# A two-layer mLSTM and retention trunk on one core: the same operations, put in order by a planner with other durations

## The chip, the cores and the metric

The kernel runs on one core of a Trainium2 chip (trn2). A core has a matrix engine (PE, with its weight loads shown as PEld), a vector engine (DVE), a scalar engine (ACT), a general engine (POOL) and a queue engine (SP), which here issues every DMA transfer. Each engine carries out its own list of instructions in order; an instruction waits until the semaphores that it names have been raised by others. The metric is the time of one execution on the device in microseconds (us), the median of several runs.

## The reference

Two layers over a sequence of T = 1024 tokens of width D = 1024, and a final RMS norm. All is float32. Per layer, cut to what matters:

```
shift, scale, gate = split(silu(c) @ w_ada[l] + b_ada[l])
h = rmsnorm(x, norm_g[l]) * (1 + scale) + shift
p = h @ w_in[l]                        # 1024 x 1024 by 1024 x 9224
mq, mk, mv, mo, mz, mi, mf, rq, rk, rv, rz = split(p)
mq, mk = silu(causal_conv4([mq, mk]))
y_m = sigmoid(mo) * head_norm(mlstm(mq, mk, mv, mi, mf)) * silu(mz)   # 4 heads of 256
y_r = head_norm(retention(rotary(rq), rotary(rk), rv)) * silu(rz)     # 4 heads of 256
x = x + gate * ([y_m, y_r] @ w_out[l])                                # 2048 x 1024
```

`mlstm` is linear attention with an exponential input gate, a sigmoid forget gate and a running maximum; its gates come from the eight columns `mi, mf`. `retention` is linear attention with a fixed decay per head.

## The kernel before

**Work.** Float32 products are taken as three products of rounded parts: every operand is split into a high part (`hH`, `wH`, `yH`, `oH`, `aH`: a copy by ACT into the matrix engine's 32-bit format) and a low part (`hL`, `wL`, ..: the difference, by DVE or POOL), and `mm3` records high by high, low by high and high by low. The projection `h @ W_in` is done for pairs of 128 columns (`pair`) by a scheme with seven instead of eight block products; the blocks of weights come from memory as `raw` tiles of 128x512, are added and subtracted by DVE and then split. Each finished pair of 128x1024 outputs (`x`) goes through what its columns need: `conv_pair` (convolution and SiLU, for q and k of the mLSTM heads), `rot_pair` (rotary, for q and k of retention), `v_pair`, and `zo_pair` or `z_pair` (gates). The results are stored to memory in `qdr` (q and k), `kdr` and `vdr` (rearranged k and v) and `gdr` (gates, two halves of the sequence), and loaded again where they are used.

**A layer in order.** First the "border": the first gate column block, the values of head group 0 and the eight gate columns (`border_gate`, `border_values`, whose results are gathered in a tile `g8`, shown as `g`), while the normed input of the layer is made. Then `gate_chain`: one long chain of small instructions over the mLSTM gates (scans, a maximum, two transposes of tiles `T4` on PE, exponentials). All mLSTM attention needs its results. Then the pairs of eight head groups (four mLSTM, then four retention); `attention(l, hg)` is recorded as soon as q and k of a group are there. It loads `q` and `kk` from `qdr`, `st` pieces from `vdr` and `kdr`, works in four chunks of 256 tokens with a carried state `cf`, and stores normed outputs `ndr`. Side jobs (`ada_column_job`, `gate_col_job`, `gate_row_job`, `rotary_job`) sum `w_ada` rows on DVE into `aacc` and put them through PE; `gate_row_job` of layer 1 splits `aacc` into `aH` and `aL` and multiplies them by `ones_r`. Last comes `output`: `yr` (from `ndr`) times `yg` (from `gdr`) is split into `yH` and `yL`, and multiplied by `w_out` tiles (`wo`, split into `oH`, `oL`) in two halves of the sequence and two halves of the columns, four 128x512 sums at a time. `evac` of layer 0 loads the residual (`hf<-in_xt_dram`), adds the sum out of its PSUM bank (`hf<-pp,gcol,hf`) and transposes it into `z`; `norm` then makes the next layer's input (`dg`). `evac` of layer 1 adds `xr`, norms and stores the output.

**What sets the order.** The code does not issue instructions where it is written. Every operation is recorded as an `Op` (`Program.record`), with a modelled duration and latency (`cost`), the operations that it depends on (`deps`) and the buffers that it allocates. `Program.order` then plays the whole program through four times (`simulate`): at each step the engine that can start earliest takes an operation. PE takes the earliest of four streams (`pre`, `sums`, `attn`, `main`), each in recorded order; DVE, ACT, POOL and SP take, of the operations whose inputs are there, the one with the smallest `late`, the latest start that the round before left it. A buffer gets a slot of its class when one is free in the model, in recorded order, up to 45 us (`LOOK`) ahead of PE. The best of the four rounds gives the order of all five engines, and the slots. At the end one loop emits all, so that nearly every instruction bears the line of that loop: L1720 in the kernel before, L1743 in the changed one.

```
for op in made:
    getattr(engines[op.eng], op.fn)(*[real(v) for v in op.a], **{n: real(v) for n, v in op.k.items()})
```

An instruction still waits on the chip for what it needs; the planned times are not kept, the order is. 16225 operations are recorded.

## Time and profile before

| | |
|---|---|
| median of 3 runs | 2313.88 us (2313.14 to 2314.32) |
| profiled execution, its own time | 2313.45 us |
| its span, first to last instruction | 2311.7 us |
| mean granted PE clock over the span | 0.974 |
| busy: PE, PEld, DVE, ACT, POOL | 2161.7, 1764.6, 1690.6, 1065.1, 189.4 us |
| DMA | 360.97 MB, mean 156 GB/s |
| table loads on ACT | 23, 1283 ns each |

The profiled execution's own time is 1.75 us above its span and 0.43 us below the median. PE's clock is granted in tenths of full speed; a stretch at half clock makes the same matmuls longer and counts as busy. So PE loses time in two ways: it is idle, or it is busy at a lower clock. The rows of the view by windows name a stretch of the span, then its length, the busy time and instructions of PE, PEld, DVE, ACT and POOL, the granted clock, the busy share of the DMA engines and GB/s. In the timeline a row has its start, its duration, engine, line, operation, out<-in, shapes, the count of equal instructions in a row, and in brackets the idle time before it with what ended it; SPq is the queue that issues the DMAs. PE's single records overlap, so that the pitch from one start to the next is shorter than a record.

### The profile page before, as it was taken

The page shows a single profiled execution, that of the slowest core. Times are in us where ns is not written, and L with a number is a line of the kernel's source. Part 1 is how long each engine was busy: PE and PEld are TensorE (multiplying, and loading weights), DVE is VectorE, ACT ScalarE, POOL GpSimd, SP SyncE. Part 2 cuts the span into 40 slices and gives each one's busy share as a digit, 9 for nine tenths or more (in the row PEclk, how much of TensorE's full clock was granted, in tenths as well). Part 3 has the DMA queues.
Part 4 walks back from the last instruction along what each step waited for, and adds up shares of the span by engine and source line. Part 5 has one row for each costly group of instructions (what it writes and reads, how often), then busy time and mean ns, then how long its engine had stood idle before and what let it go on. Part 6 is the DMA issues. An engine that isn't in the chain of part 4 may idle for free. (4 is left out here: it accounts for less than half of the span.)

```text
span 2311.7 us, 30256 instructions
## 1 busy us (share of the span) xinstructions
PE 2161.7 (94%) x9629; PEld 1764.6 (76%) x9629; DVE 1690.6 (73%) x3054; ACT 1065.1 (46%) x1938; POOL 189.4 (8%) x223
## 2 busy tenths in 40 slices
PE   3899999999999999997897999999989999999998
PEld 3788888877777787775677888788868888887776
DVE  7888889889677866654547997686868677785463
ACT  4364444644444344533345646555553444343432
POOL 1100000001000000012120000100000000000313
PEclk9899999999999999998998999999989999999999
DMA  7233434366666656666532344554554555456775
GB/s 247 70 92 109 122 118 121 107 205 195 177 171 194 168 158 163 209 214 218 197 94 73 94 127 149 162 151 133 170 157 131 144 161 138 143 179 196 207 229 154
DMA packets 490412, 360.97 MB, mean 156 GB/s; under 512 B 186098, under 2 KB 413178, under 8 KB 490252
## 3 DMA queue, kind: packets, MB, share of 16 engines
q1 hardware_dynamic: 490252, 359.04, 53.4%
q8 instruction: 76, 1.25, 0.2%
q14 instruction: 84, 0.69, 0.1%
HBM read 252.43 MB, written 106.46 MB: 155 GB/s over the span
## 5 line engine op out<-in xcount | busy, mean ns | idle before, releaser
L1720 PE MATMUL pp<-hL,wH 128*128 128x512 f32 x1968 | 789.1, 401 | 3.3 <-DVE hL L1720 2.3
L1720 PE MATMUL pp<-hH,wH 128*128 128x512 f32 x1968 | 788.9, 401 | 1.9 <-ACT wH L1720 1.2
L1720 PE MATMUL pp<-hH,wL 128*128 128x512 f32 x1968 | 786.7, 400 | 1.5 <-DVE wL L1720 1.2
L1720 ACT CAST wH<-raw 128x512 fp32r<-128x512 f32 x416 | 256.5, 619 | 437.7 <-PE pp L1720 316.3
L1720 PEld LDWEIGHTS pp<-hL,wH 128*128 128x128 f32 x1968 | 372.2, 189 | 88.9 <-DVE hL L1720 2.9
L1720 PEld LDWEIGHTS pp<-hH,wL 128*128 128x128 f32 x1968 | 372.0, 189 | 88.2 <-DVE wL L1720 4.2
L1720 PEld LDWEIGHTS pp<-hH,wH 128*128 128x128 f32 x1968 | 372.2, 189 | 85.8 <-ACT wH L1720 1.6
L1720 DVE TENSOR_TENSOR wL<-raw,wH 128x512 fp32r<-128x512 f32 x416 | 285.8, 689 | 113.3 <-ACT wH L1720 108.0
L1720 POOL TENSOR_TENSOR rsd<-va,mhalf 128x2 f32<-128x2 f32 x64 | 48.2, 753 | 1190.0 <-DVE va L1720 1054.2
L1720 ACT CAST oH<-wo 128x512 fp32r<-128x512 f32 x128 | 77.8, 616 | 138.8 <-PE pa L1720 64.2
L1720 DVE SCALAR_TENSOR_TENSOR acc<-x,cols,acc 128x1024 f32<-128x1024 f32 x96 | 122.7, 1278 | 1.9 <-ACT acc L1720 1.6
L1720 PE MATMUL pa<-cf,q 128*128 128x258 f32 (+1 forms) x384 | 109.4, 393 | 7.2 <-DVE cf L1720 6.8
L1720 PE MATMUL pa<-v,kt 128*128 128x258 f32 (+1 forms) x384 | 101.6, 388 | 0.1
L1720 POOL TENSOR_TENSOR oL<-wo,oH 128x512 fp32r<-128x512 f32 x64 | 83.6, 1307 | 211.0 <-ACT oH L1720 206.6
L1720 PEld LDWEIGHTS pa<-q,kk 128*128 128x128 f32 x512 | 77.2, 194 | 28.7 <-DMA q<-qdr 9.2
L1720 PE MATMUL pa<-q,kk 128*128 128x128 f32 (+1 forms) x512 | 84.8, 309 | 14.7 <-DMA q<-qdr 11.3
L1720 PE MATMUL pa<-v,sd 128*128 128x258 f32 (+1 forms) x320 | 90.0, 388 | 6.9 <-ACT v L1720 6.4
L1720 DVE TENSOR_TENSOR raw<-raw,raw 128x512 f32<-128x512 f32 x136 | 93.7, 689 | 3.2
L1720 PEld LDWEIGHTS pa<-cf,q 128*128 128x128 f32 x384 | 71.5, 195 | 23.2 <-DVE cf L1720 9.3
L1720 ACT ACTIVATE nr<-nd,nmu,rsd 128x256 f32<-128x256 f32 x128 | 71.4, 594 | 37.6 <-DVE nmu L1720 28.2
L1720 DVE SCALAR_TENSOR_TENSOR yL<-yg,cols,yH 128x512 fp32r<-128x512 f32 x64 | 52.2, 816 | 47.7 <-ACT yH L1720 47.3
L1720 PEld LDWEIGHTS pa<-v,kt 128*128 128x128 f32 x384 | 74.5, 195 | 13.1 <-ACT nd L1720 0.8
(228 smaller groups left out, 3302.0 us busy)
## 6 DMA issues: line engine op xcount, KB each, us to landing
raw<-in_w_in_dram SPq DMA_DIRECT2D x280, 256.0 KB
wo<-in_w_out_dram SPq DMA_DIRECT2D x128, 256.0 KB
araw<-in_w_ada_dram SPq DMA_DIRECT2D x96, 256.0 KB
qdr<-acc SPq DMA_DIRECT2D x32, 512.0 KB
q<-qdr SPq DMA_DIRECT2D x128, 128.0 KB
kk<-qdr SPq DMA_DIRECT2D x128, 128.0 KB
qdr<-x SPq DMA_DIRECT2D x32, 512.0 KB
ndr<-zt SPq DMA_DIRECT2D x128, 128.0 KB
```

What stands on the lines that cost most here:

```text
L1720: getattr(engines[op.eng], op.fn)(*[real(v) for v in op.a], **{n: real(v) for n, v in op.k.items()})
```

## The change

Only the planner is changed: what is recorded, and so every operation and its shapes, stays. These parts of it change:

- Durations and latencies in `cost`: a 128x512 operation of two tensors on DVE from 0.723 to 0.602 us, a 128x512 copy on ACT from 0.650 to 0.525 us (0.485 out of PSUM), a scan of 512 on DVE from 0.738 to 1.145 us, the time that SP needs to issue a DMA from 0.07 to 0.43 us, the latency after an instruction from 0.03 to 0.12 us.
- Transfers: instead of bytes by one rate, each transfer is served for a time that depends on the length of its contiguous runs (`serve`), and what stands before and after it is set anew.
- ACT's tables (`table`): the planner knows that Tanh and Exp, Sin, and Ln need different tables, counts 1.3 us (`TABLE`) for a switch, and takes an operation of the table that is in if one is ready that is not more than 6 us (`HOLD`) later in `late`.
- Margins: `MARGIN` from 0.25 to 0.10 and `SYNC` from 0.10 to 0.02 us. An operation that reads what the same engine wrote now waits for the full latency (`free` marks the other dependencies).

```
--- before.py
+++ after.py
@@ -183,14 +183,15 @@
 
 class Op:
     __slots__ = ("eng", "fn", "a", "k", "dur", "lat", "bytes", "deps", "allocs", "stream", "seq", "nom", "late",
-                 "start", "end", "succ", "wait", "ready", "known", "users_of")
+                 "start", "end", "succ", "wait", "ready", "known", "users_of", "serve", "table", "free")
 
 
 class Program:
     LOOK = 45.0
-    MARGIN = 0.25
-    SYNC = 0.10
-    RATE = 185e3
+    MARGIN = 0.10
+    SYNC = 0.02
+    TABLE = 1.3
+    HOLD = 6.0
     STREAMS = ("pre", "sums", "attn", "main")
 
     def __init__(self):
@@ -206,7 +207,7 @@
         op = Op()
         op.eng, op.fn, op.a, op.k = eng, fn, a, k
         op.deps, op.allocs, op.seq = set(), [], len(self.ops)
-        op.nom, op.stream, op.bytes = self.nom, None, 0
+        op.nom, op.stream, op.bytes, op.table, op.free = self.nom, None, 0, 0, set()
         out = a[0]
         outs = [x for x in (out, k.get("accum_out")) if isinstance(x, Ref)]
         ins = [x for x in a[1:] if isinstance(x, Ref)]
@@ -231,6 +232,8 @@
             if fn == "memset":
                 x.buf.cleared = op
         op.deps.discard(op)
+        data = {o for x in ins for o, area in x.buf.writes if touch(area, x.area)}
+        op.free = {o for o in op.deps if o not in data and o.eng == eng}
         self.cost(op, out, ins)
         if eng == "PE":
             op.stream = self.stream
@@ -241,36 +244,45 @@
 
     def cost(self, op, out, ins):
         eng, fn = op.eng, op.fn
-        n = max([elements(x) for x in ins + [out] if isinstance(x, Ref)] or [1])
+        refs = [x for x in ins + [out] if isinstance(x, Ref)]
+        n = max([elements(x) for x in refs] or [1])
+        wide = sum(1 for x in ins if elements(x) == 1 and n > 2)
         psum = any(x.buf.cls in ("p", "a") for x in ins)
-        op.lat = 0.03
+        op.lat = 0.12
         if fn == "dma_start":
-            o = out if isinstance(out, Ref) else ins[0]
+            o = next(x for x in refs if not x.buf.dram)
             total = 4
             for s in o.shape:
                 total *= s
-            op.bytes, op.dur = total, (0.95 if eng == "POOL" else 0.07)
+            run = 4 * min(x.shape[-1] for x in list(op.a[:2]) if len(x.shape))
+            op.bytes, op.dur = total, (0.95 if eng == "POOL" else 0.43)
+            op.serve = 1.07e-3 * total / run * (9 + 0.0375 * run) / 16
         elif eng == "PE":
             n = elements(out)
-            op.lat = 0.18
+            op.lat = 0.20
             if fn == "transpose":
                 op.dur = 0.109
             elif op.a[1].dt == F32R:
-                op.dur = max(0.075, 0.005 + 0.000443 * n)
+                op.dur = max(0.064, 0.004 + 0.000444 * n)
             else:
                 op.dur = max(0.222, 0.004 + 0.00167 * n)
         elif eng == "DVE":
             if fn == "tensor_tensor_scan":
-                op.dur = 0.2 + 0.00105 * n
+                op.dur = 0.07 + 0.0021 * n
             elif fn in ("tensor_scalar", "tensor_copy", "memset") and not psum:
-                op.dur = 0.19 + 0.00053 * n
+                op.dur = 0.07 + 0.00052 * n
+            elif fn == "transpose":
+                op.dur = 0.10 + 0.00104 * n
             else:
-                op.dur = 0.185 + 0.00105 * n
+                op.dur = 0.07 + 0.00104 * n
+            op.dur += 0.06 * wide
         elif eng == "ACT":
-            wide = fn == "activation" and (isinstance(op.k.get("scale"), Ref) or isinstance(op.k.get("bias"), Ref))
-            op.dur = 0.22 + (0.0011 if wide else 0.00084) * n
+            op.dur = (0.055 if psum else 0.095) + 0.00084 * n + 0.095 * wide
         else:
-            op.dur = 0.7 if len(op.a) > 3 and op.a[3] == ALU.pow else 0.35 if fn == "affine_select" else 0.2 + 0.00225 * n
+            op.dur = 0.70 if len(op.a) > 3 and op.a[3] == ALU.pow else 0.45 if fn == "affine_select" else 0.16 + 0.00225 * n
+        if eng == "ACT" and fn == "activation":
+            f = op.a[2]
+            op.table = 1 if f in (AF.Tanh, AF.Exp) else 2 if f == AF.Sin else 3 if f == AF.Ln else 0
 
     def order(self, rounds):
         ops = self.ops
@@ -320,7 +332,7 @@
         free = dict.fromkeys(engines, 0.0)
         ready = {e: [] for e in engines}
         pending = {e: [] for e in engines}
-        server = [0.0]
+        server, table = [0.0], [0]
         streams = {s: [o for o in ops if o.eng == "PE" and o.stream == s] for s in self.STREAMS}
         at = dict.fromkeys(self.STREAMS, 0)
         head = dict.fromkeys(queues, 0)
@@ -407,7 +419,7 @@
                 else:
                     continue
                 if e == "SP":
-                    t = max(t, server[0] - 5.0)
+                    t = max(t, server[0] - 4.5)
                 if best is None or t < best:
                     best, pick = t, (e, None)
             if pick is None:
@@ -433,12 +445,23 @@
                     o = heapq.heappop(pending[e])[2]
                     heapq.heappush(ready[e], (o.late, o.seq, o))
                 op = heapq.heappop(ready[e])[2]
+                if e == "ACT" and op.table not in (0, table[0]):
+                    same = [x for x in ready[e] if x[2].table in (0, table[0]) and x[0] < op.late + self.HOLD]
+                    if same:
+                        heapq.heappush(ready[e], (op.late, op.seq, op))
+                        x = min(same)
+                        ready[e].remove(x)
+                        heapq.heapify(ready[e])
+                        op = x[2]
+                    else:
+                        table[0] = op.table
+                        t += self.TABLE
             op.start = t
             free[e] = t + op.dur
             if op.bytes:
-                begin = max(t + op.dur + 0.9, server[0])
-                server[0] = begin + op.bytes / self.RATE
-                op.end = server[0] + 1.0
+                begin = max(t + op.dur + 0.85, server[0])
+                server[0] = begin + op.serve
+                op.end = server[0] + 0.4
             else:
                 op.end = t + op.dur + op.lat
             last = max(last, op.end)
@@ -447,7 +470,7 @@
                 if op.bytes:
                     t1 = op.end + (self.MARGIN if o.eng == "PE" else 0.0)
                 elif o.eng == op.eng:
-                    t1 = op.start + op.dur
+                    t1 = op.start + op.dur if o.eng == "PE" or op in o.free else op.end
                 else:
                     t1 = op.end + self.SYNC + (self.MARGIN if o.eng == "PE" else 0.0)
                 o.ready = max(o.ready, t1)
```

The new order and the slots that go with it differ in many places (1351 of 4699 buffers get another slot). Three are shown; numbers in a name belong to the buffer, and with the second number of a name the two kernels differ where nothing else does.

The first place is the end of layer 0, where the gates of the last head group are stored and the residual is loaded. SP's rows before (`x_2189` and `x_2194` are the last two gate tiles, `hf_2202` is the residual of the fourth output tile, whose sum is in the bank `pp_2207`):

```order
L1720 DMA yg_2462_10268<-gdr_54_5395 128x512
L1720 DMA ndr_34_9914<-zt_2143_9698 32x8x128
L1720 DMA gdr_64_10271<-x_2189_9095 128x512
L1720 DMA gdr_66_10273<-x_2194_9141 128x512
L1720 DMA hf_2382_10276<-in_xt_dram 128x512
L1720 DMA yr_2468_10282<-ndr_30_8648 128x512
L1720 DMA yg_2469_10285<-gdr_56_6542 128x512
L1720 DMA yr_2475_10291<-ndr_30_8648 128x512
L1720 DMA hf_2202_10293<-in_xt_dram 128x512
```

and now:

```order
L1743 DMA gdr_64_9537<-x_2189_9330 128x512
L1743 DMA yr_2316_9543<-ndr_33_9358 128x512
L1743 DMA gdr_66_9554<-x_2194_9383 128x512
L1743 DMA yg_2317_9562<-gdr_65_9498 128x512
L1743 DMA hf_2199_9487<-in_xt_dram 128x512
L1743 DMA wo_2292_9576<-in_w_out_dram 128x512
L1743 DMA hf_2200_9491<-in_xt_dram 128x512
L1743 DMA hf_2201_9511<-in_xt_dram 128x512
L1743 DMA hf_2202_9597<-in_xt_dram 128x512 x2
```

This stood at rows 769 to 777 of SP's list, with the loads of `yr` and `yg` of a later step ahead of `hf_2202`'s; it stands at rows 757 to 765 now, with the residuals together. On DVE the emptying of the bank `pp_2207` into `hf_2202` stood there before:

```order
L1720 SCALAR_TENSOR_TENSOR yL_2457_10280<-yg_2455_10260,cols0_137_278,yH_2456_10278 128x512
L1720 TENSOR_TENSOR yg_2462_10268<-yr_2461_10266,yg_2462_10268 128x512
L1720 SCALAR_TENSOR_TENSOR yL_2464_10289<-yg_2462_10268,cols0_137_278,yH_2463_10287 128x512
L1720 SCALAR_TENSOR_TENSOR hf_2382_10276<-pa_2329_9862,gcol_143_6571,hf_2382_10276 128x512
L1720 TENSOR_TENSOR yg_2469_10285<-yr_2468_10282,yg_2469_10285 128x512
L1720 SCALAR_TENSOR_TENSOR yL_2471_10307<-yg_2469_10285,cols0_137_278,yH_2470_10303 128x512
L1720 SCALAR_TENSOR_TENSOR hf_2202_10293<-pp_2207_9205,gcol_143_6571,hf_2202_10293 128x512
```

and now:

```order
L1743 TENSOR_TENSOR oL_2315_9792<-wo_2313_9690,oH_2314_9787 128x512
L1743 SCALAR_TENSOR_TENSOR hf_2199_9487<-pp_2204_9444,gcol_143_7338,hf_2199_9487 128x512
L1743 SCALAR_TENSOR_TENSOR hf_2200_9491<-pp_2205_9454,gcol_143_7338,hf_2200_9491 128x512
L1743 STREAM_TRANSPOSE z_2321_9879<-hf_2199_9487 128x512
L1743 SCALAR_TENSOR_TENSOR hf_2201_9511<-pp_2206_9464,gcol_143_7338,hf_2201_9511 128x512
L1743 SCALAR_TENSOR_TENSOR hf_2202_9597<-pp_2207_9474,gcol_143_7338,hf_2202_9597 128x512
L1743 TENSOR_TENSOR sqs_2320_9873<-sqs_2320_9873,o_2322_9882 128x512
```

It was behind a row of products of the output phase's later steps (`yg`, `yL`), and now stands right behind its sisters of the same sums.

The second place is the gate chain of layer 0 on PE, the first transposes of `T4`. Before (in row 1922 of PE's list):

```order
L1720 MATMUL pp_1356_4218<-hH_298_621,wH_1357_4108 128x512
L1720 MATMUL pp_1356_4218<-hL_299_654,wH_1357_4108 128x512
L1720 MATMUL pa_418_4237<-ident_1_86,T4_410_1120 128x128 x4
L1720 MATMUL pp_1356_4218<-hH_298_621,wL_1358_4120 128x512
L1720 MATMUL pp_1346_4131<-hH_280_577,wH_1360_4142 128x512
```

and now (row 992):

```order
L1743 MATMUL pp_843_2436<-hH_277_565,wH_844_2336 128x512
L1743 MATMUL pp_843_2436<-hL_278_579,wH_844_2336 128x512
L1743 MATMUL pa_418_2452<-ident_1_76,T4_410_1116 128x128 x4
L1743 MATMUL pp_843_2436<-hH_277_565,wL_845_2351 128x512
L1743 MATMUL pp_843_2436<-hH_295_615,wH_844_2336 128x512
```

The transposes moved forward by 930 rows of PE's list, to among the products of an earlier pair, and the mLSTM attention, which needs them, with them.

The third place is the gate row job of layer 1 on ACT, ahead of the copy `aH`. Before:

```order
L1720 ACT_TABLE_LOAD
L1720 ACTIVATE rot_3647_15585<-rot_3647_15585 128x512
L1720 ACT_TABLE_LOAD
L1720 ACTIVATE x_3631_15648<-x_3631_15648 128x512
L1720 CAST wH_3664_15656<-raw_3650_15532 128x512
L1720 CAST aH_3643_15671<-aacc_3632_15415 128x512
L1720 ACT_TABLE_LOAD
L1720 ACTIVATE rot_3648_15633<-rot_3648_15633 128x512
L1720 CAST wH_3669_15680<-raw_3667_15594 128x512
```

and now:

```order
L1743 CAST wH_3659_15836<-s1_3653_15587 128x512
L1743 ACTIVATE nd_3559_15812<-pa_3565_15817,wd_155_2641 128x258
L1743 ACTIVATE th_3630_15857<-x_3625_15851 128x512
L1743 CAST aH_3643_15883<-aacc_3632_15368 128x512
L1743 ACTIVATE nr_3573_15903<-nd_3559_15812,nmu_3571_15898,rsd_3570_15885 128x256 x2
L1743 CAST wH_3662_15911<-raw_3606_15184 128x512
L1743 ACTIVATE th_3630_15857<-x_3625_15851 128x512
L1743 ACTIVATE nd_3578_15923<-pa_3579_15849,wd_155_2641 128x258
L1743 ACTIVATE nd_3578_15923<-pa_3581_15880,wd_155_2641 128x258
L1743 ACT_TABLE_LOAD
L1743 ACTIVATE rot_3648_15901<-rot_3648_15901 128x512
```

The copy `aH_3643` had two table loads and a rotary tile (`rot`) closely ahead of it; now the next table load comes six rows behind it.

More of the change, by code (lines that the diff above doesn't have):

```diff
@@ L185 @@
     __slots__ = ("eng", "fn", "a", "k", "dur", "lat", "bytes", "deps", "allocs", "stream", "seq", "nom", "late",
-                 "start", "end", "succ", "wait", "ready", "known", "users_of")
+                 "start", "end", "succ", "wait", "ready", "known", "users_of", "serve", "table", "free")
 class Program:
     LOOK = 45.0
-    MARGIN = 0.25
-    SYNC = 0.10
-    RATE = 185e3
+    MARGIN = 0.10
+    SYNC = 0.02
+    TABLE = 1.3
+    HOLD = 6.0
     STREAMS = ("pre", "sums", "attn", "main")
@@ L233, in record @@
         op.deps.discard(op)
+        data = {o for x in ins for o, area in x.buf.writes if touch(area, x.area)}
+        op.free = {o for o in op.deps if o not in data and o.eng == eng}
         self.cost(op, out, ins)
@@ L435, in simulate @@
                 op = heapq.heappop(ready[e])[2]
+                if e == "ACT" and op.table not in (0, table[0]):
+                    same = [x for x in ready[e] if x[2].table in (0, table[0]) and x[0] < op.late + self.HOLD]
+                    if same:
+                        heapq.heappush(ready[e], (op.late, op.seq, op))
+                        x = min(same)
+                        ready[e].remove(x)
+                        heapq.heapify(ready[e])
+                        op = x[2]
+                    else:
+                        table[0] = op.table
+                        t += self.TABLE
             op.start = t
@@ L449, in simulate @@
                 elif o.eng == op.eng:
-                    t1 = op.start + op.dur
+                    t1 = op.start + op.dur if o.eng == "PE" or op in o.free else op.end
                 else:
```

45 lines of the change are left out of this document (27 added, 18 removed).

## The prediction

> **What bounds the kernel now.** I read the page first, for which engine is full and where it is not.
>
> ```profile
> span 2311.7 us, 30256 instructions
> PE 2161.7 (94%) x9629; PEld 1764.6 (76%) x9629; DVE 1690.6 (73%) x3054; ACT 1065.1 (46%) x1938; POOL 189.4 (8%) x223
> PEclk9899999999999999998998999999989999999999
> ```
>
> PE is the bound: 94% busy, and no operation on it is removed. So an order can give back only PE's idle time, 2311.7 - 2161.7 = 150.0 us, and what it lost while its clock stood lower. Next, the view of waits on PE: what it waited for, us in total, how often, the longest.
>
> ```profile
> PE pa L1720 <- DVE aacc L1720: 26.7, 4, 13.0
> PE pa L1720 <- DVE g L1720: 16.0, 2, 12.3
> PE pp L1720 <- DVE hf L1720: 15.7, 1, 15.7
> PE pa L1720 <- DMA q<-qdr: 11.3, 6, 4.8
> PE pp L1720 <- ACT aH L1720: 8.6, 2, 4.8
> PE pp L1720 <- ACT oH L1720: 7.9, 4, 3.8
> PE pa L1720 <- DVE dg L1720: 6.9, 1, 6.9
> PE pa L1720 <- DVE cf L1720: 6.8, 8, 1.4
> PE pa L1720 <- ACT v L1720: 6.4, 2, 4.8
> ```
>
> There is no one cause: a few long waits and many short ones. So I cut the span by the view of windows at the places of these waits. Columns: window, length, busy PE, PEld, DVE, ACT, POOL with counts, granted clock, DMA share, GB/s.
>
> ```profile
> 0.00:100.00 100.00, 58.24 (x289) 47.88 (x290) 83.78 (x166) 43.38 (x92) 17.28 (x17) 0.93 0.57 174
> 100.00:110.00 10.00, 6.29 (x38) 5.70 (x37) 7.41 (x24) 2.48 (x6) 0.00 (x0) 0.83 0.20 57
> 110.00:460.00 350.00, 350.00 (x1551) 285.85 (x1551) 305.29 (x483) 183.03 (x280) 3.52 (x6) 1.00 0.37 109
> 460.00:1025.00 565.00, 534.35 (x2392) 437.50 (x2390) 413.91 (x861) 250.13 (x507) 37.99 (x61) 0.98 0.65 185
> ...
> 1080.00:1102.00 22.00, 6.33 (x21) 4.72 (x20) 12.47 (x19) 6.10 (x10) 0.00 (x0) 0.61 0.88 289
> 1145.00:1163.00 18.00, 6.10 (x12) 3.61 (x12) 11.96 (x19) 9.17 (x13) 1.18 (x1) 0.62 0.36 127
> 1239.00:1256.00 17.00, 4.71 (x24) 4.08 (x23) 13.14 (x31) 3.66 (x7) 0.00 (x0) 0.60 0.12 35
> 1440.00:1675.00 235.00, 231.00 (x1032) 189.28 (x1031) 182.74 (x357) 129.67 (x240) 14.53 (x31) 1.00 0.54 154
> 1675.00:1735.00 60.00, 51.39 (x212) 41.56 (x211) 41.21 (x91) 32.37 (x59) 4.03 (x7) 0.89 0.55 155
> 1735.00:2020.00 285.00, 285.00 (x1280) 235.31 (x1280) 210.12 (x362) 115.04 (x219) 7.23 (x11) 1.00 0.51 145
> 2020.00:2165.00 145.00, 137.59 (x595) 109.34 (x594) 93.64 (x164) 61.92 (x115) 13.06 (x13) 0.99 0.64 192
> 2165.00:2260.00 95.00, 89.33 (x372) 70.58 (x371) 53.41 (x78) 36.55 (x67) 23.03 (x20) 0.96 0.74 216
> 2260.00:2312.00 52.00, 43.63 (x189) 35.03 (x187) 16.02 (x24) 15.11 (x31) 17.33 (x16) 0.95 0.54 146
> ```
>
> I call loss of a window its length less PE's busy time, plus (1 - clock) times the busy time. For 460 to 1025 that is 30.65 + 0.02 x 534.35 = 41.3 us. In the order of the rows: 45.8, 4.8, 0, 41.3, 18.1, 14.2, 14.2, 4.0, 14.3, 0, 8.8, 9.2, 10.6: together 185 us, the most that any order could find here. Each step below asks what the new order does to one of these.
>
> **The change, step by step.**
>
> *(a) End of layer 0, 1080 to 1102, loss 18.1.* The timeline shows what PE waited for, and SP's queue ahead of it:
>
> ```profile
> 1098.03 0.80 PE L1720 MATMUL pp<-yH,oH 128*128 128x512 f32 x1 [15.66 <-DVE hf L1720]
> 1086.78 1.14 SPq L1720 DMA_DIRECT2D gdr<-x  x2
> 1096.16 0.46 SPq L1720 DMA_DIRECT2D hf<-in_xt_dram  x1
> ```
>
> PE needs the bank that `hf_2202` empties. Its residual was issued at 1096.16, 9.4 us behind the last gate stores, since loads of `yr` and `yg` stood between them that wait for slots, and on DVE the emptying stood behind the products that use these. In the new lists the residuals stand together, and the emptying right behind its sisters. Neither the store nor the work is new; only what is queued between. I take the whole loss, 18; bounds 0 and 18.1. What is late next is the last gate's product itself, that the old order also had to wait for.
>
> *(b) Attention of layer 0, 460 to 1025, loss 41.3.* These are the waits for `q`, `cf` and `v`. By the view of one tile (ns of one, then first and last start and the forms):
>
> ```profile
> L1720 PE MATMUL pa<-ident,T x16: 270/272/300, 479.4 to 1418.2; 128*128 128x128 f32 x16
> L1720 PE MATMUL pa<-q,kk x512: 270/275/796, 495.4 to 2126.4; 128*128 128x128 f32 x127, 128*128 128x256 f32 x44
> ```
>
> No attention ran before 495.4, since the gate chain's transposes came at 479.4. The attention of all eight groups was pressed into the 565 us behind; ahead of it stand 350 us without one idle moment. The new list has the transposes 930 rows earlier, and each group's attention follows its production. Layer 1 shows what attention spread in this way costs: its windows lose 4.0 (1440 to 1675), 0 (1735 to 2020) and 8.8 (2020 to 2165), 12.8 us. So I take 41.3 - 12.8 = 28 (bounds 0 and 41.3).
>
> *(c) Gate row job, 1675 to 1735, loss 14.3.*
>
> ```profile
> 1682.68 0.80 PE L1720 MATMUL pp<-aH,ones_r 128*128 128x512 f32 x1 [4.79 <-ACT aH L1720]
> 1677.73 1.28 ACT L1720 ACT_TABLE_LOAD   x1
> 1679.67 1.28 ACT L1720 ACT_TABLE_LOAD   x1
> ```
>
> Two table loads and a rotary tile stood ahead of the copy; there are none now, 2.6 us and more. PE's list has 18 instructions between the last product and the use of `aH` (12 at the second half), where it had none: 18 x 350/1551 = 4.1 us of cover for a wait of 4.79, 2.7 for the second, 8.6 - 4.8 = 3.8. Both together would leave about 1; I take 9 of 14.3, since the attention's copies now stand ahead of `aH` on ACT (bounds 0 and 14.3). The number of table loads is the same in both lists, 23, so the table rule itself is worth nothing more than where they stand.
>
> *(d) 2020 to 2165, loss 8.8.* The last attentions stand 154 PE rows earlier, 154 x 0.226 = 35 us. 5 (0 to 8.8). *(e) 2165 to 2260, loss 9.2*, waits for `oH` and `xr`: loads are issued in another order, but stores of the first half's output now stand ahead of some `wo` loads on SP and may hold them up. 4 (-4 to 9.2).
>
> *(f) 100 to 110, loss 4.8*, the tile `g8`:
>
> ```profile
> 100.15 0.69 DVE L1720 TENSOR_TENSOR wL<-raw,wH 128x512 fp32r<-128x512 f32 x1 [1.04 <-ACT wH L1720]
> 103.26 0.30 DVE L1720 MEMSET g<- 128x288 f32 x1
> 1154.20 4.87 DVE L1720 TENSOR_TENSOR hf<-hf,pa 128x512 f32<-128x512 f32 x8 [2.17 <-PE pa L1720]
> ```
>
> Three DVE instructions fewer stand ahead of its memset: 3 x 4.87/8 + 1.04 = 2.9, and with its share of the clock 2.9 x 4.8/3.71 = 3.7 (0 to 4.8). *(g) Border norm, 1145 to 1163*: two DVE instructions fewer ahead of `dg`, 1 (0 to 2). *(h)* The second `g8`, 1239 to 1256, the first 100 us and the tail have nearly the same lists: 0 (each within 3), as 1440 to 1675.
>
> **What it adds.** *(i) DVE in the first 300 us.* From row 130 of both lists to the transposes of `T4`, DVE has 313 instructions and PE 879 now; before 565 and 1809. At the rates of 110 to 460 (305.29/483 = 0.632 and 0.226) that is 198 us on either engine now, and 357 against 409 before. DVE had 52 us to spare and has none. If it idled as in that window, 13%, 198/0.872 - 198 = 29 us would be lost; if that idling was just its slack, 0. PE was 100% busy there, so DVE's idling held up nothing: nearer to 0, I take -5 (0 to -29). *(j) SP's issue.* The planner now counts 0.43 us for a DMA; the trace shows more in a burst:
>
> ```profile
> 606.49 4.88 SPq L1720 DMA_DIRECT2D st<-vdr  x8
> 611.47 0.38 SPq L1720 DMA_DIRECT2D st<-kdr  x1
> ```
>
> (611.47 - 606.49)/8 = 0.62. A chunk of attention issues some 22 DMAs, so its last piece may come 22 x 0.19 = 4 us later than planned; the old plan, with 0.07, was further off and the loss came to the waits of (b). -4 (0 to -12).
>
> DVE's 0.602 for a 128x512 operation fits the pitch of 4.87/8 = 0.609; the old 0.723 did not. That is why the new list dares to fill DVE early.
>
> Sum: 18 + 28 + 9 + 5 + 4 + 3.7 + 1 - 5 - 4 = 59.7 us less than the profiled execution's 2313.45 (its span and 1.75), so 2254; the median shown stands 0.43 above that.
>
> A rule on the clock bears on (b). The row of one such place:
>
> ```profile
> 564.00:576.00 12.00, 9.21 (x39) 7.15 (x38) 10.56 (x28) 4.30 (x9) 0.70 (x1) 0.86 0.61 204
> 876.00:888.00 12.00, 7.21 (x23) 5.99 (x23) 5.33 (x11) 2.52 (x5) 0.70 (x1) 0.72 0.58 161
> ```
>
> At 564 to 576 PE was idle for 2.8 us in all and the clock fell to 0.86. The Trainium skill, "TensorE: Matmul & The Clock Gate", Part 1: The HAM clock gate, has the clock halve only after a whole window of about 3.4 us of idleness. By that rule this fall has another cause than the pauses, and would stay; the trace speaks against it here. What this would give is the fourth rival.
>
> **The rivals.**
>
> 1. *Attention is spread, but waits elsewhere* (b gives 0): the queue of loads, 65% of DMA time busy in that window, is no less full. For it: the waits for `cf` are for DVE, which gets no less work. Against: layer 1's 12.8. 2254 + 28 = 2282.
> 2. *All of it goes*, and nothing is added: 41.3 + 18.1 + 14.3 + 8.8 + 9.2 + 4.8 + 1.2 = 97.7, so 2216. For it: the windows at 1735 and 110 show no loss over 285 and 350 us. Against: two windows of layer 1 lose 4.0 and 8.8 although DVE is idle for a quarter of them and more.
> 3. *Slower: each head group meets a queue that is late.* SP is in order: a load that waits for a slot or a store holds up all behind it, as in (a). The row of 876 shows the price of one such wait for `q`: 4.79 + 0.28 x 7.21 = 6.8 us. The gains without (i) and (j) are 68.7; 68.7/6.8 = 10.1, so it decides from eleven of the sixteen groups on, and with all sixteen 2313.45 + 108.8 - 68.7 = 2354. For it: the list is made with an issue time that bursts exceed. Against: before, with 0.07, six waits for `q` cost 11.3 in all.
> 4. *The low clock in (b) stays*: 0.02 x 534.35 = 10.7 less gain, 2265.
> 5. *It does nothing*: what is moved is moved by a planner that the chip doesn't follow, and the gains are paid back. About 2313.
>
> **How the numbers follow.** Forecast 2254: 0.55, its own range 2235 to 2275, from the bounds of (a) to (j) taken as independent. Rival 1: 0.16. Rival 2: 0.11. Rival 3: 0.09. Rival 4: 0.05. Rival 5: 0.04. A difference of 0.2%, 4.6 us, is about what a measurement of this kernel can tell from none. Faster: 0.55 + 0.16 + 0.11 + 0.05 = 0.87; the same 0.04; slower 0.09. The range reaches down to rival 2 (2215) and up to rival 1 with half of the further cost in (i) and (j), 2282 + 0.5 x (24 + 8) = 2298; outside lie rivals 3 and 5 and the far sides of 1 and 2, about 0.2.
>
> **What would show it.** (a): no wait of `pp` for `hf` over 2 us at the end of layer 0. (b): the first `q,kk` matmul at about 250 to 300 us, and the waits for `q`, `cf` and `v` at about a third. (c): no wait for `aH` over 2 us. (d), (e): waits for `oH` shorter. (i): a new row of waits for `wL` or `hL` from 110 to 300 us would show DVE as the bound there. (j): waits for `q` or `kk` of 1 to 4 us at each group. The largest waits left should be those for `aacc` in the first 100 us and `g` in 1239 to 1256, with 12 to 13 us each. The prediction is wrong if the middle of layer 0 loses as much as before, or if the first 300 us lose more than 20 us to DVE.

## The result, and the profile after

The changed kernel takes 2324.89 us (median of 6 runs, 2321.97 to 2329.70) against 2314.1 us: the ratio is 1.0047 with an interval of 1.0033 to 1.0061. It is half a per cent slower, where 2254 us was forecast. The profiled execution took 2324.77 us. The page of the kernel after:

```profile
span 2323.0 us, 30234 instructions
PE 2168.3 (93%) x9629; PEld 1758.8 (76%) x9629; DVE 1673.7 (72%) x3054; ACT 1057.0 (45%) x1938; POOL 186.0 (8%) x223
PEclk9899999999999999999899999999999999999999
```

PE is idle for 2323.0 - 2168.3 = 154.7 us, 4.7 more than before, and its busy time is 6.6 us longer. The view of PE's waits shows that these are other waits (us in total, times, longest):

```profile
PE pa L1743 <- DMA kk<-qdr: 31.4, 18, 4.3
PE pa L1743 <- DVE aacc L1743: 16.2, 3, 8.9
PE pa L1743 <- DVE g L1743: 10.0, 2, 9.7
PE pa L1743 <- DVE sqs L1743: 9.3, 1, 9.3
PE pa L1743 <- DMA q<-qdr: 8.8, 12, 1.7
...
PE pa L1743 <- DVE T L1743: 6.5, 3, 4.2
PE pa L1743 <- ACT kt L1743: 5.1, 9, 1.3
...
PE pa L1743 <- DVE dg L1743: 2.7, 1, 2.7
PE pp L1743 <- ACT aH L1743: 2.7, 1, 2.7
```

The wait of 15.7 us for `hf` is gone, those for `oH` too, and those for `aH`, `dg` and `g` are shorter. In their place PE waits 30 times, 40.2 us, for `q` and `kk`; before it was 12.9 us. The windows show where (window, its length, PE busy, and so on as before). First the kernel before, in stretches that were not shown:

```profile
250.00:1025.00 775.00, 744.35 (x3301) 608.19 (x3300) 600.04 (x1142) 357.44 (x672) 40.99 (x66) 0.98 0.58 166
1025.00:1140.00 115.00, 99.13 (x416) 79.68 (x417) 57.29 (x79) 38.75 (x63) 22.64 (x18) 0.91 0.66 213
1260.00:2020.00 760.00, 747.39 (x3339) 614.11 (x3339) 586.70 (x1043) 377.52 (x681) 34.52 (x60) 0.99 0.50 143
```

and after:

```profile
110.00:250.00 140.00, 138.38 (x599) 112.12 (x600) 135.17 (x230) 73.30 (x110) 3.60 (x6) 1.00 0.38 108
250.00:1025.00 775.00, 732.37 (x3222) 591.50 (x3221) 577.65 (x1109) 353.09 (x668) 32.87 (x60) 0.98 0.59 169
1025.00:1140.00 115.00, 105.67 (x451) 85.66 (x450) 55.15 (x76) 37.43 (x61) 24.00 (x19) 0.96 0.56 182
1260.00:2020.00 760.00, 731.28 (x3223) 590.45 (x3222) 570.22 (x1013) 365.95 (x665) 33.60 (x59) 0.99 0.50 140
```

At the end of layer 0 (1025 to 1140) the idle time fell from 15.9 to 9.3 us. In the stretches in which the head groups are produced and attention runs beside them it rose, from 30.7 to 42.6 us in layer 0 and from 12.6 to 28.7 us in layer 1. I call these two the group stretches below; their idle time together went from 43.3 to 71.3 us, 28.0 more. In the rest of the span it fell by 23.3 us (from 106.7 to 83.4). The border of the layers came at the same time as before, by the rows of the norm's product (before, then after):

```profile
L1720 PE MATMUL pa<-dg,ones_r x4: 590/828/1222, 1152.1 to 1211.8; 128*128 128x512 f32 x4
L1743 PE MATMUL pa<-dg,ones_r x4: 592/592/697, 1152.5 to 1211.2; 128*128 128x512 f32 x4
```

So in layer 0 gains and losses cancel to 0.4 us, and layer 1 lost the rest.

One such wait close by, in the timeline of PE and of SP's queue:

```profile
406.94 0.59 PE L1743 MATMUL pa<-q,kk 128*128 128x256 f32 x2
410.51 1.89 PE L1743 MATMUL pa<-q,kk 128*128 128x256 f32 x7 [2.97 <-DMA kk<-qdr]
...
404.85 0.34 SPq L1743 DMA_DIRECT2D qdr<-acc  x1
405.29 1.91 SPq L1743 DMA_DIRECT2D raw<-in_w_in_dram  x2
407.77 0.82 SPq L1743 DMA_DIRECT2D kk<-qdr  x2
```

PE had products of the projection to do, but attention's matmul stood ahead of them in its list. The load of `kk` was issued at 407.77, 2.9 us behind the store of what it loads, and PE went on 2.74 us later. SP waits for such stores itself, and all behind them in its list waits with it; the view of SP's waits has a row for it that the kernel before has not:

```profile
SPq L1743 <- DMA qdr<-acc: 24.4, 14, 3.3
```

The view of DMA issues gives the times from issue to landing for all transfers of a kind (the last column is their median, us):

```profile
qdr<-acc SPq DMA_DIRECT2D x32, 512.0 KB, 2.6
q<-qdr SPq DMA_DIRECT2D x128, 128.0 KB, 2.7
kk<-qdr SPq DMA_DIRECT2D x128, 128.0 KB, 2.8
...
st<-vdr SPq DMA_DIRECT2D x448, 32.0 KB, 2.2
```

The new planner counts 0.43 + 0.85 + 0.41 + 0.40 = 2.09 us for a load of `kk` (issue, begin, service, end), the old one 0.07 + 0.90 + 0.71 + 1.00 = 2.68. So the new plan has the data of these loads 0.6 to 0.7 us earlier than the chip (not of every transfer: for the 512 KB store `qdr<-acc` it counts 3.07 us, where the chip took 2.6), and where a burst of loads stands ahead, earlier still: attention's small loads follow each other on SP at 0.474 us in the median and at 0.52 us in the mean of the changed kernel's trace (pauses over 3 us left out), and the plan has 0.43. The part of a transfer that does not grow with its bytes is 0.43 + 0.85 + 0.40 = 1.68 us in the new plan and 1.97 in the old one. The Trainium skill, "DMA: Bandwidth & Descriptors", Anatomy of one DMA, gives about 2.0 us for that part, most of it the wait for the completion, though for transfers that the general engine issues. The 2.2 us of a 32 KB load here agree with it, and speak against the new number.

### The profile page after: what moved, and what is told of

It is laid out like the page before. It is cut to its first block, busy times and chain, and to the rows that moved or that the text cites. A ratio compares the mean times of both kernels' runs of the same rounds, so it can differ in the third digit from the quotient of the medians.

```text
span 2323.0 us, 30234 instructions
## 1 busy us (share of the span) xinstructions
PE 2168.3 (93%) x9629; PEld 1758.8 (76%) x9629; DVE 1673.7 (72%) x3054; ACT 1057.0 (45%) x1938; POOL 186.0 (8%) x223
## 5 line engine op out<-in xcount | busy, mean ns | idle before, releaser
L1743 PE MATMUL pa<-q,kk 128*128 128x128 f32 (+1 forms) x512 | 93.3, 327 | 45.4 <-DMA kk<-qdr 31.4
L1743 PEld LDWEIGHTS pa<-v,kt 128*128 128x128 f32 x384 | 71.4, 191 | 24.5 <-ACT kt L1743 10.7
L1743 DVE TENSOR_TENSOR yg<-yr,yg 128x512 f32<-128x512 f32 x64 | 50.5, 789 | 51.7 <-DMA yg<-gdr 51.6
```

## The experiments

All edits are in the planner, and the lists were planned again. The kernel before was timed beside each group, 2312.3 to 2314.0 us; the ratios are to it.

| run | edit | us | ratio, interval | idle in the group stretches |
|---|---|---|---|---|
| (the change) | | 2324.9 | 1.0047, 1.0033 to 1.0061 | 71.3 |
| e1 | arrival as before | 2302.3 | 0.9951, 0.9936 to 0.9966 | 56.8 |
| e2 | margins as before | 2311.1 | 0.9990, 0.9979 to 1.0001 | 62.3 |
| e3 | both | 2278.5 | 0.9852, 0.9833 to 0.9871 | 48.2 |
| e4 | control | 2326.9 | 1.0059, 1.0039 to 1.0078 | 72.4 |
| e5 | issue 0.48 | 2289.1 | 0.9898, 0.9883 to 0.9913 | 52.3 |
| e6 | e3 and issue 0.48 | 2249.6 | 0.9730, 0.9714 to 0.9746 | 24.5 |
| e7 | old durations of DVE, ACT | 2329.5 | 1.0071, 1.0056 to 1.0086 | 67.4 |
| e8 | issue 0.07 | 2458.5 | 1.0631, 1.0616 to 1.0647 | 139.4 |
| e9 | issue 0.55 | 2262.8 | 0.9785, 0.9767 to 0.9802 | 36.0 |
| e10 | room everywhere | 2206.1 | 0.9541, 0.9526 to 0.9556 | 6.4 |
| e11 | old transfer rate | 2300.2 | 0.9944, 0.9927 to 0.9962 | 37.8 |
| e12 | no table rule | 2342.2 | 1.0131, 1.0115 to 1.0147 | 79.3 |
| e13 | issue 0.70 | 2242.3 | 0.9693, 0.9677 to 0.9709 | 22.8 |
| e14 | wide margins | 2278.3 | 0.9851, 0.9833 to 0.9869 | 44.2 |
| e15 | kernel before with e10's room | 2310.3 | 0.9984, 0.9973 to 0.9994 | 35.4 |
| e16 | e10 with old durations | 2227.0 | 0.9630, 0.9616 to 0.9644 | 15.2 |

The last column is 775 + 760 us less PE's busy time, from two window rows of each run. The windows are the same times in every run, so in a list that is much shorter or longer they cut the work a little elsewhere; over the whole span PE is idle for 74.3 us in e10 and for 248.3 us in e8, against 154.7 after the change.

### Arrival, margins, or scatter

e1, against the changed kernel:

```diff
-                begin = max(t + op.dur + 0.85, server[0])
+                begin = max(t + op.dur + 0.9, server[0])
-                op.end = server[0] + 0.4
+                op.end = server[0] + 1.0
```

> The changed planner with one of its edits undone: a transfer begins 0.9 us behind its issue and is taken as landed 1.0 us behind its service (as before), not 0.85 and 0.4. That makes a planned 128 KB load of q or kk 2.74 us long from issue to landing instead of 2.09; the trace of the changed kernel has 2.7 to 2.8. All else stays new, and the lists are planned again. Theory A (arrival: the new plan puts attention's matmuls 0.65 us ahead of their data, PE waits in order): the waits of PE for q and kk fall from 40.2 us (30 times) to 13 or less, the sum of the kernel before, and with the low clock behind them the time falls by 27 to 40 us, to 2285 to 2298. Theory B (margins: what is missing is the slack that MARGIN and SYNC gave every dependency): under 10 us less, 2315 or more, with the waits for ACT's kt, nd, cf, v as they are. Theory C (DVE: its list is full since its durations were cut): no change, 2320 to 2328. Theory D (scatter: any other list would give some other time): anything within 15 us either way.

Measured: 2302.3 us, 22.6 less than the changed kernel and less than the kernel before. The waits for the two loads fell, but not to 13:

```profile
PE pa L1743 <- DMA kk<-qdr: 16.8, 15, 2.1
...
PE pa L1743 <- DMA q<-qdr: 10.1, 11, 2.3
```

So the arrival is a part of it, smaller than theory A had it.

e2:

```diff
-    MARGIN = 0.10
-    SYNC = 0.02
+    MARGIN = 0.25
+    SYNC = 0.10
```

> The changed planner with its two margins undone: MARGIN 0.25 and SYNC 0.10 as before, not 0.10 and 0.02; the arrival of transfers stays new. A data dependency of PE on another engine then has 0.23 us more slack, one on a transfer 0.15. Theory A: a quarter of the missing 0.65 us for transfers, so 7 to 10 us less, about 2316, with waits for q and kk of 30 us still. Theory B: most of the loss comes back, 25 us or more, 2300 or less, and the many short waits (kt, nd, cf, v, 14 us together) are gone. Theory C: 2320 to 2328.

2311.1 us, 13.8 less: between what A and B expected. C, no change, fell with these two.

e3 has both edits.

> Both edits undone: the arrival of transfers as before and MARGIN 0.25, SYNC 0.10. Theory A: as with the arrival alone, a few us less, 2280 to 2295. Theory B: as with the margins alone, 2300 or less. If both are at work in different waits, the two gains add up: 35 to 50 us less, 2275 to 2290. Theory C: 2320 to 2328.

2278.5 us, 46.4 less, ten more than the two gains added. It is now 1.5% faster than before.

e4:

```diff
-    SYNC = 0.02
+    SYNC = 0.021
```

> A control on scatter: the changed planner with SYNC 0.021 instead of 0.02, a difference of 1 ns that no instruction on the chip knows of, but that may tip ties in the plan. Theories A, B and C: the time of the changed kernel within 4 us, 2321 to 2329. Theory D: 2310 to 2340, as far off as the other variants.

2326.9 us, 2 from the changed kernel. This control says little on theory D, since its list is nearly the same: 74 of PE's 8779 operations stand elsewhere, and 1405 in e5. What speaks against scatter is the order of the results: over five issue times in the plan (0.07 to 0.70 us, below) each longer one gave a faster kernel, and so did each step of more room in e3, e6 and e10.

### The time to issue a DMA

e5:

```diff
-            op.bytes, op.dur = total, (0.95 if eng == "POOL" else 0.43)
+            op.bytes, op.dur = total, (0.95 if eng == "POOL" else 0.48)
```

> The changed planner with one number set otherwise: SP takes 0.48 us to issue a DMA instead of 0.43 (the trace of the changed kernel has five issues in 2.43 us). Arrival and margins stay new. Theory J (a burst of SP issues is later than planned, so loads at its end come late): some 22 issues per chunk of attention are 1.1 us late at their end now and would not be; waits for q and kk 25 us instead of 40 and 8 to 20 us less time, 2305 to 2317. Rival, theory A alone (only the end of a transfer counts): within 5 us of the changed kernel, 2320 to 2330.

2289.1 us: 0.05 us in one number gave 35.7 us, where 8 to 20 were expected, and more than arrival or margins. The waits for `q` and `kk` fell to 24.0 us, as expected. The chip does the same operations; only the order differs.

e6 is e3 with 0.48.

> The kernel with the arrival and the margins undone (2278.5) and 0.48 us for an issue besides. It still waits 18.9 us for q and kk. Theory J: half of that and of its low clock goes, 10 to 25 us less, 2253 to 2268. Rival: what is left are waits for other things (the sum aacc, cf, g), 2274 to 2282.

2249.6 us, somewhat better than expected. PE's waits for these loads are down to 9.3 us:

```profile
PE pa L1743 <- DMA kk<-qdr: 5.4, 10, 1.2
...
PE pa L1743 <- DMA q<-qdr: 3.9, 4, 1.6
```

e8 goes the other way, to the old 0.07 (and the old window of 5.0 for the queue):

```diff
-            op.bytes, op.dur = total, (0.95 if eng == "POOL" else 0.43)
+            op.bytes, op.dur = total, (0.95 if eng == "POOL" else 0.07)
-                    t = max(t, server[0] - 4.5)
+                    t = max(t, server[0] - 5.0)
```

> The changed planner with the old issue time of SP, 0.07 us (and the old window of 5.0 us); all else new. Theory J: loads are planned into bursts that SP needs seven times as long for; 22 of them end 8 us late, once or more in each of the 16 head groups: 50 to 150 us more, 2375 to 2475, nearly all of it waits for q, kk and for kt and v behind them. Rival (the kernel before also counted 0.07 and waited only 12.9 us for q and kk, so that the number does not matter): 2310 to 2335.

2458.5 us, 133.6 more, as theory J expected. Waits on PE:

```profile
PE pa L1743 <- DMA kk<-qdr: 54.9, 19, 6.3
PE pa L1743 <- DMA q<-qdr: 37.3, 12, 6.3
PE pa L1743 <- DVE cf L1743: 23.2, 12, 3.1
```

e9 and e13 set 0.55 and 0.70, more than the queue takes.

> As the kernel with 0.48 us for an issue (2289.1), but 0.55, more than the trace's pitch of 0.47 to 0.49 within a run of equal issues; arrival and margins stay new. Theory J (what counts is that the number is not below the real pitch): within 8 us of 2289, 2281 to 2297. Rival (any slack on the queue is worth its length, right or wrong): the gain from 0.43 to 0.48 was 36 us, so from 0.48 to 0.55 some 25 to 50 us more, 2240 to 2265.

> As the kernels with 0.48 and 0.55 us for an issue (2289.1, 2262.8), but 0.70, far above what the queue takes. In the traces the pitch of attention's small loads is 0.474 in the median and 0.52 in the mean, since one in ten is held up. Theory J (the number must reach the real mean pitch; beyond it nothing is to be had): 2255 to 2275. Theory R (room: every tenth of a us by which the plan lets data come later than they do takes waits away): 0.15 us more than 0.55 is twice the step from 0.48 to 0.55, which gave 26; with less left to gain, 20 to 40 us less, 2222 to 2243.

2262.8 and 2242.3 us: 26.3 and another 20.5 less. Theory J fell here. It is not the right number that counts; each further step away from the real one still gave time, though less for each tenth of a us. Theory R's range for 0.70 (2222 to 2243) holds, at its edge.

### Room

e10 takes e6 further:

```diff
-    MARGIN = 0.10
-    SYNC = 0.02
+    MARGIN = 0.5
+    SYNC = 0.3
-            op.bytes, op.dur = total, (0.95 if eng == "POOL" else 0.43)
+            op.bytes, op.dur = total, (0.95 if eng == "POOL" else 0.52)
-                begin = max(t + op.dur + 0.85, server[0])
+                begin = max(t + op.dur + 0.9, server[0])
-                op.end = server[0] + 0.4
+                op.end = server[0] + 1.3
```

> The best kernel so far (arrival and margins as before, issue 0.48: 2249.6) with more room still: issue 0.52, a transfer landed 1.3 us behind its service, MARGIN 0.50, SYNC 0.30. If PE's waits in the head groups are the plan's lack of room: the 9.3 us for q and kk and 8 us for cf and kt that it still has go, 8 to 15 us less, 2235 to 2242. If room costs time once the numbers are right: 2250 to 2265.

2206.1 us, far below the 2235 to 2242 expected, and the best of all: 4.6% faster than before. Its page, its waits on PE and its group stretches:

```profile
span 2204.3 us, 30161 instructions
PE 2130.0 (97%) x9629; PEld 1748.7 (79%) x9629; DVE 1673.6 (76%) x3054; ACT 1064.3 (48%) x1936; POOL 203.7 (9%) x223
```

```profile
PE pa L1743 <- DVE aacc L1743: 20.6, 2, 11.0
PE pa L1743 <- DVE g L1743: 12.4, 3, 9.9
...
PE pa L1743 <- DMA kk<-qdr: 0.7, 2, 0.5
PE pa L1743 <- DMA q<-qdr: 0.7, 1, 0.7
```

```profile
250.00:1025.00 775.00, 772.72 (x3485) 635.35 (x3485) 600.14 (x1138) 377.55 (x701) 61.90 (x76) 1.00 0.64 184
1260.00:2020.00 760.00, 755.89 (x3390) 620.76 (x3389) 587.69 (x1073) 377.83 (x699) 35.79 (x58) 1.00 0.56 160
```

Of 1535 us only 6.4 are idle. What is left are the long waits at the beginning and at the border of the layers, which no list of this study took away. From the changed kernel to this one the span is 118.7 us shorter: 80.4 of it idle time (154.7 to 74.3), and 38.3 in which PE counted as busy, with the same operations. My expectation had only counted waits that were left, not that others went with them.

e14 widens the two margins alone (0.50 and 0.30).

> The changed planner with MARGIN 0.50 and SYNC 0.30 alone; issue 0.43 and the arrival of transfers stay new. A transfer has 0.40 us more room before PE, any other dependency of PE 0.68. The old margins (0.15 and 0.23 more) gave 14 us. Theory R: two to three times that, 28 to 45 us less, 2280 to 2297. If only the queue counts (theory J): 2305 to 2315, no better than the old margins, with waits for q and kk over 30 us.

2278.3 us, 46.6 less, just beyond the good end of theory R's range. Room that is not on the queue works too, though 24.2 us of waits for `q` and `kk` stay (13.4 and 10.8).

e15 gives the same room to the planner of the kernel before (the five numbers of e10, all else old).

> The planner of the kernel before, with its old durations and transfer rate and without table rule, given the room of the best kernel so far (issue 0.52, landed 1.3 us behind the service, MARGIN 0.50, SYNC 0.30). If room is all that a plan here needs: well below 2313, 2230 to 2270. If the old plan has room enough already, by its long durations (0.12 us in each DVE and ACT instruction, and 1.42 us of service for a 256 KB load), and loses its time in late attention and in the long waits: 2300 to 2320.

2310.3 us: next to nothing. Its group stretches are idle for 35.4 us, and its long waits are of the kind that the new lists had taken away:

```profile
PE pp L1720 <- DVE hf L1720: 11.4, 1, 11.4
PE pp L1720 <- DVE oL L1720: 10.3, 14, 3.2
PE pa L1720 <- DVE x L1720: 10.2, 2, 9.6
PE pa L1720 <- DVE dg L1720: 10.0, 1, 10.0
PE pp L1720 <- ACT aH L1720: 8.9, 2, 4.8
```

So room alone does not make the old plan better, and the new numbers alone did not either. The length that a planner gives its own list (`planned` in `Program.order`) fits this: 2372.7 us in the kernel before and 2421.4 in e15, 61 and 112 us longer than the chip took; 2168.3 in the changed one, 155 us shorter than the chip; 2185.7 in e10, 19 us shorter. The change made the plan 204 us shorter and the kernel 11 us longer.

e16 is e10 with the old durations of DVE and ACT.

> The best kernel so far (2206.1) with the old durations of DVE and ACT; its room, its transfers and its table rule stay. What the new durations are worth once there is room: undone without room they changed the time by 5 us. If right durations bring attention forward, as it was forecast for this change: 15 to 40 us more, 2221 to 2246. If durations are only another form of room: 2200 to 2212.

2227.0 us, 21 more than e10, as expected if right durations bring something once there is room. Its first attention matmul comes at 392.2 us, in e10 at 255.7, which fits the expectation's reason. From e15 to e16 it is 83 us; what differs there, above all the service time of a transfer, the table rule, the latencies and the wait for what the same engine wrote, was not separated.

### The other parts of the change, undone without room

e7 puts back the old durations of DVE and ACT (their branches of `cost`).

> The changed planner with the old durations of DVE and ACT (0.723 and 0.650 us for 512 columns; traces have 0.609 and 0.525); arrival, margins and issue stay new. Each such instruction then has 0.12 us of padding. Theory C (without padding DVE's list is full, and what it is late with stops PE): 10 to 20 us less, 2305 to 2315, with the waits for cf, kt, nd, v gone. Rival (right durations are right, padding makes the plan put PE's work later than it could run): 10 to 40 us more, 2335 to 2365. If only transfers matter: 2320 to 2330.

2329.5 us, 4.6 more. The time lies in the last range, but transfers alone are not the reason: the waits for `q` and `kk` fell from 40.2 to 21.2 us, and `g` and `cf` rose instead (from 10.0 to 23.2 and from 2.5 to 13.5). Attention began at 474.2 us again, as in the kernel before (495.4), so it is these durations that brought it forward.

e11:

```diff
-            op.serve = 1.07e-3 * total / run * (9 + 0.0375 * run) / 16
+            op.serve = total / 185e3
```

> The changed planner with the old price of a transfer (bytes at 185 GB/s, not by the length of its runs); issue, arrival, margins and durations stay new. A 512 KB store then counts 2.83 us of service instead of 1.39 and a 128 KB load 0.71 instead of 0.41, so loads have 0.3 us more room behind them, half of what theory A says is missing: 10 to 15 us less, 2310 to 2315. Rival (the service time is right, and padding it makes the plan hold work back): 2335 to 2350.

2300.2 us, 24.7 less, more than expected. The old rate is longer for most transfers, and the waits for `q` and `kk` fell to 7.6 us: the cut of the service time had taken room as well. Against that stand waits of 19.7 us for `oH` and 10.5 for `dg`, of the kind that the old lists have.

e12 lets a switch of ACT's table cost nothing (`TABLE = 0.0`, `HOLD = -1.0`).

> The changed planner without its rule for ACT's tables (a switch costs nothing and nothing is held back for it); all else new. Before and after have 23 table loads each of 1283 ns. If the rule only moved them: 2320 to 2330 with 20 to 26 loads. If the rule keeps loads out of the plan without padding: some 20 loads more of 1.28 us, 26 us of ACT time of which most meets PE's waits, 2335 to 2350.

2342.2 us, 17.3 more, with 23 loads as before. The time of the second range came, but not its reason: the rule saves no loads. Why their place is worth 17 us stays open.

## Why the prediction was wrong

**Step (j) was mis-sized, and with it (b).** The prediction put SP's issue at -4 us, 12 at most: the lateness of one chunk of attention, counted once, though there are 64 chunks (two layers, eight groups, four each). Its reason was that the old number, 0.07, was further off, with its loss already in the waits of (b). The runs show 35.7 us less time with 0.48 alone and 62.1 less with 0.55, on either side of the mean pitch of 0.52 us. The reason failed too: what an old number did in the old plan says nothing of the new one, because the change took slack out of the other numbers at the same time. With 0.07 the new planner gives 2458.5 us. Undone alone, the arrival was worth 22.6 us, the margins 13.8, the transfer rate 24.7. The prediction saw none of these as a cost: the section on the change lists `MARGIN`, `SYNC` and what stands around a transfer, and the prediction priced only the issue. Which of the old numbers covered the old issue time in the kernel before was not separated.

**(b) Attention of layer 0**, +28 forecast. The first attention matmul came at 277.0 us, as forecast (250 to 300). The waits of PE for `cf` and `v` from 250 to 1025 fell, from 11.1 to 3.0 us, but those for `q` and `kk` rose from 9.7 to 23.1, and the stretch is idle for 42.6 us instead of 30.7. Layer 1 as the measure for spread attention was the wrong witness: it was quiet in the old plan, and in the new one its own idle time rose from 12.6 to 28.7 us. In e10, where the early attention has room, the idle time of that stretch in layer 0 is 2.3 us. The gain was there, but not in this plan: as far as e7 shows it, early attention without room was worth little (with attention late again it is only 4.6 us slower). For the middle of layer 1 the prediction had no cost at all, 0 beside the gain of (c); the runs show 16.1 us more idle time there.

**Rival 3, slower by a late queue, is the nearest to what happened.** Its place was right: SP waits for stores (24.4 us for `qdr<-acc`), and of the waits for `q` or `kk` of 1 to 4 us that the prediction named as the sign of (j), 30 came, some shorter and the longest 4.3. Its price, with a chance of 0.09, was not: 2354 us, from sixteen waits of 6.8 us. Many short ones did it, and the queue was not their only cause, since wider margins alone (e2, e14) took part of the loss away too.

**(a)** The wait for `hf` went, as forecast. But the norm of the first half, which stood behind it, then waited 9.3 us for `sqs`, whose sums DVE makes among the output phase's products. The idle time of 1025 to 1140 fell by 6.5 us, not by 16. **(c)** `aH`: 8.6 to 2.7 us, and 1.6 for `aL`: 4.3 of idle time came back, half of the forecast. **(d)** brought nothing: the last attention matmul came 6.7 us earlier, not 35, and 2020 to 2165 is idle for 7.3 us as before (7.4). **(e)** the waits for `oH` are gone, and from 2165 on 10.3 us are idle instead of 13.7. **(f)** `g` lost its first wait but for 0.3 us, 16.0 to 10.0 in all. **(g)** `dg`: 6.9 to 2.7, more than forecast. **(h)** the second wait for `g` stayed, 12.3 to 9.7; `aacc`, forecast to stay, fell from 26.7 to 16.2. **(i)** DVE did not become the bound in the first 250 us: PE is idle for 1.6 us from 110 to 250, at the good end of 0 to -29, with DVE busy for 135.2 of the 140.

**The range** took (j) and (b) as nearly independent and ended at 2298. Both hang on the same thing, how late data may be in the new plan, so they failed together.

## What to carry to other kernels

A plan from measured durations is made for a chip on which nothing is late; where one in-order engine serves several streams, every dependency then stops it for what the model lacks. Put the true durations in, and add room behind each dependency and transfer on purpose, and try more of it until the time rises, which no run here reached: here 0.7 us of it behind what PE waits for, 1.4 for transfers, turned a loss of 0.5% into a gain of 4.6%. Room without the new numbers gave 0.2% (e15). When a change corrects several numbers of a planner at once, ask of each whether its error had been slack for another, and do not read from the old profile that a wrong number did no harm.

## What was not expected of the hardware

Median latencies are poor plan numbers for a queue that issues in bursts: the pitch of small loads has its median at 0.474 and its mean at 0.52 us, since for about one in ten the next follows only after more than 0.6 us. What holds these up was not separated.

The clock did not fall after each pause. A wait for `kk` in the timeline of the changed kernel, and window rows around it and around the one at 410.51:

```profile
329.39 0.81 PE L1743 MATMUL pa<-q,kk 128*128 128x128 f32 x4 [2.28 <-DMA kk<-qdr]
...
325.00:335.00 10.00, 7.61 (x37) 5.85 (x36) 4.33 (x16) 5.76 (x15) 1.21 (x3) 1.00 0.57 151
404.00:416.00 12.00, 9.03 (x40) 7.61 (x39) 9.30 (x15) 3.47 (x8) 0.00 (x0) 0.86 0.76 222
```

The first holds a pause of 2.28 us and stays at full clock; the second holds the pause of 2.97 us at 410.51 and has 0.86. Cut finer, the clock stands at full speed through most of that pause and at half behind it:

```profile
408.00:411.00 3.00, 0.49 (x2) 0.50 (x3) 2.54 (x4) 0.95 (x2) 0.00 (x0) 0.98 0.94 292
411.00:414.00 3.00, 3.00 (x14) 2.92 (x14) 0.93 (x2) 0.00 (x0) 0.00 (x0) 0.50 0.99 269
```

So 0.86 is a mean. The section on the profile before has the clock granted in tenths of full speed; that is not so here. The clock records of all these traces hold only 1.00 and 0.50, and the tenths of the page's line are means over its slices. The Trainium skill, "TensorE: Matmul & The Clock Gate", Part 1: The HAM clock gate, has the clock halved after at least one idle window of about 3.4 us, counted by a window that runs free. The trace agrees that shorter pauses can pass without it, and differs in that a pause below 3 us was enough once; so the fourth rival's reading, that such falls have another cause than pauses, found no support, and with the pauses gone in e10 the clock is 1.00 in both group stretches.
